# State-space layer: decay rows on 96 partitions, copied to DRAM a group at a time; the first group's TensorE order written out; a fourth state row buffer

## The chip, the cores and the metric

The kernel runs on one core of one Trainium2 chip. The metric is the device time of one execution in microseconds (us), the median over runs. Five engines work at once, each through its own instructions in order: TensorE (PE, matrix products; its weight loads are PEld), VectorE (DVE), ScalarE (ACT), GpSimd (POOL) and SyncE (SP, which issues nearly all DMAs here). An engine waits for another through semaphores.

## What is computed

The reference is a trunk of two layers, each a half-step feed-forward, a token mixer and another half-step feed-forward with normalisations. All 512 tokens have width 1024. The change lies in the mixer of the first layer, a bidirectional state-space scan over 32 heads in 4 groups of 8, in its chunked form:

```python
proj = u @ w_in
z, xbc, dt_raw = jnp.split(proj, [D_INNER, D_INNER + CONV_CH], axis=-1)
xbc = jax.nn.silu(depthwise_conv(xbc, conv_w, conv_b))
...
dt = jax.nn.softplus(dt_raw.astype(f32).reshape(b, t, 2, SSM_HEADS) + dt_bias.astype(f32))
A = -jnp.exp(a_log.astype(f32))
...
a_cs = jnp.cumsum(a, axis=-1)
L = jnp.exp(segsum(a))
CB = jnp.einsum('bclgn,bcsgn->bgcls', Cc, Bc)
y_diag = jnp.einsum('bgcls,bgjcls,bcsgjp->bclgjp', CB, L, Xc)
...
y_off = jnp.einsum('bclgn,bcgjpn,bgjcl->bclgjp', Cc, states, jnp.exp(a_cs))
```

In the kernel, a head's decay matrix L is made as exp(row + bias), where row is a cumulated decay over the tokens (one for each direction) and bias holds the same for the other token index with the log of dt. The kernel uses two chunks of 256 tokens, for both directions in one matrix E.

## The kernel before

Features lie on the 128 partitions, tokens along the free dimension. Every projection is a sum of three fp32r products (high and low parts of weights and inputs); `proj` calls `mm3`, and all their matmuls stand at L176. A projection unit of the state-space layer is 24 matmuls of 512 tokens into one PSUM bank (tile acc).

The function `ssm` has these steps, in this order.

- `dt_chain` makes the steps and cumulated decays: `pcs` (L710) is copied to `cs` (ACT, L716), `bias` (tile ssbias) is the difference (DVE, L717), four transposes (PE, L720) turn cs into rows, one for each head and direction. ACT copies 64 rows into `rows` (L722), and writes the exponentials that the state term needs into `rowe` (L724, L725). Four DMAs (L729) copy everything, for 32 heads, 16 times over into the DRAM tile `scr`.
- `prepare(g)` builds a group's shared matrices: `cb` (C times B, L796), `xt` (transposed inputs, L804 and L806), `xd` (inputs times decay, DVE, L809) and two states (PE, L813, evicted by ACT into `st`, L815).
- `ssd_head(h)` reads a head's rows back, broadcast over the partitions: `rw` (two directions, DMA at L823, two buffers) and `ch` (the state row, L825, three buffers, times C on DVE, L826). POOL masks them (L840).
- `ssd_mats(h, c)` makes E for a head and a chunk: four ACT exponentials (L848 to L851), one POOL addition (L854), one DVE multiplication by cb (L855). E has five buffers.
- `ssd_out` multiplies: three products for each of two heads into one bank (PE, tile mid, L865): two with E, one with ch and st. This is called a run below. A run appears in the trace as 12 records, since each fp32 product has two.

The loop over a group's `s` from 0 to 7 handles a pair of heads in two steps, one for each chunk: at even s it calls `ssd_head` for both heads, at each s `ssd_mats` and `ssd_out`. Between the steps it emits projection units for the next group from the list `todo` (in the first group: two convolution units for B and C, four for x, two for z), whose results ACT and DVE evict (`conv`: xc at L740, L743, L746). `last_exp` keeps an eviction xc behind the exponentials that were emitted before it.

The order on each engine is set by a scheduler that takes the emitted program, the tiles' dependences and the NOSYNC edges that the code adds. Before the change nothing ties the runs of products to a place on PE.

The text speaks of pairs 1 to 4 of the first group, each with a first run (chunk 0) and a second run (chunk 1).

Of the kernel before, what the change touches and what calls it, by code (L numbers as in the profile page):

```python
# [9 lines left out]
F32 = mybir.dt.float32  # L10
# [36 lines left out]
def hybrid_trunk(tc, xT, cb, par, cst, adaw, wgu, wdn0, wdn1, wdn2, wdt, win, wso, wqk, wv, wao, dist_in, dtp, lam_in, out):  # L47
# [114 lines left out]
    last_mm, gate = [None], [None]  # L162
# [9 lines left out]
    def mm3(o, terms, after=None, start=True):  # L172
        n, j, last = 3 * len(terms), 0, None
        for wh, wl, uh, ul in terms:
            for a, b in ((wh, uh), (wh, ul), (wl, uh)):
                last = nc.tensor.matmul(o, lhsT=a, rhs=b, start=start and j == 0, stop=j == n - 1, skip_group_check=not start)  # L176
# [473 lines left out]
    def ssm(n):  # L650
# [13 lines left out]
        scr = dp.tile([16, 32, 3, T], F32, name="scr")  # L664
# [8 lines left out]
        def dt_chain(pd):  # L673
# [41 lines left out]
            cs = tmp("cs")[:, :W]  # L715
            nc.scalar.activation(cs, pcs[:, :W], AF.Copy)  # L716
            nc.vector.tensor_tensor(out=bias.rearrange("p i h -> p (i h)"), in0=lu, in1=cs, op=ALU.subtract)  # L717
# [60 lines left out]
        def prepare(g, xs, bc):  # L778
# [19 lines left out]
            for c in range(2):  # L798
                pst = acc("ln")
                for o in range(2):  # L800
                    i = 2 * c + o
                    pp = acc("ln")
                    for k in range(4):
# [7 lines left out]
                        in1=dd[:, i, g * 8 : (g + 1) * 8].unsqueeze(2).broadcast_to([P, 8, 64]), op=ALU.mult,  # L811
# [7 lines left out]
        def ssd_head(h, Ct):  # L819

            src = scr[:, h].unsqueeze(1)
            rw = ep.tile([P, 2, T], F32, tag="rw", name="rw")
            nc.sync.dma_start(rw, src[:, :, 0:2].broadcast_to([16, 8, 2, T]))  # L823
            ch = ep.tile([P, T], F32, tag="ch", name="ch", bufs=3)
# [20 lines left out]
        def ssd_mats(h, c, rw, dx, cbs):  # L845
            E = ep.tile([P, T], F32, tag="E", name="E", bufs=NE)
            i = 2 * c
            nc.scalar.activation(E[:, :W], rw[:, 0, c * W : (c + 1) * W], AF.Exp, bias=bias[:, i, h : h + 1])  # L848
            nc.scalar.activation(E[:, W:], rw[:, 1, c * W : (c + 1) * W], AF.Exp, bias=bias[:, i + 1, 32 + h : 33 + h])
            nc.scalar.activation(dx[:, c, 0, :], dx[:, c, 0, :], AF.Exp, bias=bias[:, i, 32 + h : 33 + h])  # L850
            e = nc.scalar.activation(dx[:, c, 1, :], dx[:, c, 1, :], AF.Exp, bias=bias[:, i + 1, h : h + 1])  # L851
# [3 lines left out]
            nc.vector.tensor_tensor(out=E, in0=E, in1=cbs[c], op=ALU.mult)  # L855
            return E

        def ssd_out(pr_, c, py, mats, chs, xt, states):
            cc = slice(c * W, (c + 1) * W)
            col = [slice(pr_ * P + hh * 64, pr_ * P + (hh + 1) * 64) for hh in range(2)]  # L860
            for k in range(3):
                for hh in range(2):
                    lhs = xt[2 * c + k][:, col[hh]] if k < 2 else states[1 - c][:, col[hh]]
                    rhs = mats[hh][:, k * W : (k + 1) * W] if k < 2 else chs[hh][:, cc]
                    nc.tensor.matmul(py[hh * 64 : (hh + 1) * 64, cc], lhsT=lhs, rhs=rhs, start=k == 0, stop=k == 2)  # L865
# [59 lines left out]
        for g in range(NG):  # L925
# [263 lines left out]
def _layout(i):  # L1189
# [12 lines left out]
    def unit(w):  # L1202
# [15 lines left out]
    A["par"] = par  # L1218
    A["dtp"] = cc(np.concatenate(
        [rows(np.tile(f[k][0].reshape(-1), 4)) for k in ("ssm_dt_bias", "ssm_a_log")], axis=1  # L1220
# [26 lines left out]
    A["wdt"] = cc(w[:, 5120:].reshape(KT, P, 64).transpose(1, 0, 2).reshape(P, 512))  # L1247
# [37 lines left out]
```

## Time and profile before

| | us |
|---|---|
| median of 3 runs | 2162.59 (2161.16 to 2165.55) |
| the profiled execution, its own time | 2160.72 |
| its span | 2158.9 |
| TensorE clock granted, mean | 0.995 |

| stretch | us from the span's start |
|---|---|
| first copy of rows to DRAM issued | 416.4 |
| first masks on POOL | 436.8 |
| first exponential of a decay matrix | 444.3 |
| first run of products | 457.7 |
| first transpose for the second group | 510.3 |
| last record of the products at L865 | 750.9 |

Views of the profile give rows of this kind. A timeline row is start, length, engine, line, operation, output<-inputs, shapes, and in brackets the idle time ahead and what ended it. A chain row is start, length and work. A wait row is who waited for whom, total, times, longest. Matmuls overlap: a matmul of 512 tokens lasts 0.39 us in its row, and the next starts 0.23 us after it.

### The profile page before, as it was taken

What the parts mean: (1) busy time and instruction counts of PE and PEld (TensorE: products, weight loads), DVE (VectorE), ACT (ScalarE), POOL (GpSimd) and SP (SyncE); (2) the same over time, 40 slices, a digit from 0 to 9 for tenths busy, and PEclk for the clock granted to TensorE, in tenths of its full rate; (3) what the DMA queues carried; (4) which work ended last, traced back from release to release, by engine and by line L of the source; (5) the groups of instructions that cost most, each with busy time, mean ns of one, the idle gap of its engine ahead of it and who ended that gap; (6) DMA issues with size and microseconds to landing.
All of it is one profiled execution on the core that took longest, in us unless ns stands there. A gap on an engine that the chain in (4) does not pass through costs nothing.

```text
span 2158.9 us, 34079 instructions
## 1 busy us (share of the span) xinstructions
PE 2113.4 (98%) x13230; PEld 1854.8 (86%) x13230; DVE 1761.3 (82%) x2924; ACT 1088.2 (50%) x1824; POOL 159.5 (7%) x258
## 2 busy tenths in 40 slices
PE   7999999999999999999999999999999999999997
PEld 6889899866777698999999989899888878989897
DVE  6979998556666798989988988997777878958796
ACT  5424354757655646334456434353866647424343
POOL 0000000045333300000000000000111100000000
PEclk9999999999999999999999999999999999999999
DMA  9863635474445452636443272723322312423231
GB/s 322 307 214 113 229 120 178 102 194 139 139 135 149 119 157 79 228 124 206 152 131 118 82 260 96 258 93 112 99 69 79 89 59 69 137 78 114 73 118 40
DMA packets 90083, 301.20 MB, mean 140 GB/s; under 512 B 10048, under 2 KB 13504, under 8 KB 89920
## 3 DMA queue, kind: packets, MB, share of 16 engines
q1 hardware_dynamic: 88384, 294.81, 42.1%
q0 software_dynamic: 1536, 4.20, 0.9%
q8 instruction: 104, 1.70, 0.3%
q14 instruction: 59, 0.48, 0.1%
HBM read 289.53 MB, written 5.24 MB: 137 GB/s over the span
## 4 chain that ended last, share of the span: by engine, by line
PE 82%; DVE 7%; issue 4%; ACT 3%; DMA 2%; POOL 2%; POOLq 0%; SPq 0%; ACTq 0%; DVEq 0%
PE acc L176 66%; PE mid L176 10%; PE mid L865 2%; PE ln L176 1%; PE mid L1046 1%; DMA raw<-in_wdn 1%; DVE wl L124 1%; POOL E L854 1%; DVE raw L195 1%; DMA raw<-in_wgu 1%; ACT wh L123 1%; ACT p L1056 0%; PE ln L813 0%; PE ln L1068 0%; DVE wal L116 0%
## 5 line engine op out<-in xcount | busy, mean ns | idle before, releaser
L176 PE MATMUL acc<-hi,wh 128*128 128x256 f32 (+1 forms) x1568 | 522.5, 335 | 2.8 <-ACT hi L153 1.7
L176 PE MATMUL acc<-hi,wl 128*128 128x256 f32 (+1 forms) x1568 | 522.8, 334 | 0.0
L176 PE MATMUL acc<-lo,wh 128*128 128x256 f32 (+1 forms) x1568 | 521.8, 333 | 0.3 <-DVE lo L154 0.2
L176 PE MATMUL acc<-uh,wh 128*128 128x256 f32 (+1 forms) x1160 | 391.5, 338 | 0.0
L176 PE MATMUL acc<-ul,wh 128*128 128x256 f32 (+1 forms) x1160 | 390.4, 337 | 0.0
L176 PE MATMUL acc<-uh,wl 128*128 128x256 f32 (+1 forms) x1160 | 389.2, 336 | 0.0
L123 ACT ACTIVATE wh<-raw 128x1024 fp32r<-128x1024 f32 (+1 forms) x210 | 212.8, 1021 | 256.2 <-DMA raw<-in_wdn 100.3
L527 ACT ACTIVATE wh<-raw 128x1024 fp32r<-128x1024 f32 x198 | 209.1, 1059 | 250.6 <-PE acc L176 116.2
L176 PEld LDWEIGHTS acc<-hi,wh 128*128 128x128 f32 x1568 | 295.9, 189 | 37.5 <-ACT hi L153 4.7
L176 PEld LDWEIGHTS acc<-lo,wh 128*128 128x128 f32 x1568 | 296.1, 189 | 30.8 <-DVE lo L154 2.3
L176 PEld LDWEIGHTS acc<-hi,wl 128*128 128x128 f32 x1568 | 296.1, 189 | 29.5 <-issue 0.5
L124 DVE TENSOR_TENSOR wl<-raw,wh 128x1024 fp32r<-128x1024 f32 (+1 forms) x210 | 247.4, 1182 | 46.5 <-ACT wh L123 45.2
L528 DVE TENSOR_TENSOR wl<-raw,wh 128x1024 fp32r<-128x1024 f32 x198 | 241.0, 1219 | 22.8 <-ACT wh L527 21.9
L176 PEld LDWEIGHTS acc<-uh,wh 128*128 128x128 f32 x1160 | 219.1, 189 | 29.8 <-issue 7.4
L176 PEld LDWEIGHTS acc<-ul,wh 128*128 128x128 f32 x1160 | 219.4, 189 | 25.3 <-issue 3.9
L176 PEld LDWEIGHTS acc<-uh,wl 128*128 128x128 f32 x1160 | 219.4, 189 | 24.3 <-issue 3.0
L537 DVE TENSOR_TENSOR raw<-raw 128x512 f32<-128x512 f32 x264 | 181.3, 688 | 5.1 <-DMA raw<-in_wgu 0.4
L195 DVE SCALAR_TENSOR_TENSOR raw<-raw,cond 128x1024 f32<-128x1024 f32 x144 | 173.9, 1219 | 10.7 <-DMA raw<-in_adaw 10.6
L401 DVE SCALAR_TENSOR_TENSOR resid<-acc,gv,resid 128x512 f32<-128x512 f32 (+1 forms) x156 | 104.5, 672 | 71.2 <-PE acc L176 70.7
L341 POOL TENSOR_TENSOR rr<-vr,mhalf 128x2 f32<-128x2 f32 x12 | 9.2, 766 | 1515.5 <-DVE vr L337 1515.5
L176 PE MATMUL mid<-uh,wh 128*128 128x256 f32 (+2 forms) x332 | 99.8, 302 | 0.7 <-DVE up L569 0.7
L176 PE MATMUL mid<-uh,wl 128*128 128x256 f32 (+2 forms) x332 | 99.3, 299 | 0.0
(267 smaller groups left out, 3954.5 us busy)
## 6 DMA issues: line engine op xcount, KB each, us to landing
raw<-in_wgu SPq DMA_DIRECT2D x176, 512.0 KB, 4.1
raw<-in_adaw SPq DMA_DIRECT2D x144, 512.0 KB, 4.8
raw<-in_wdn SPq DMA_DIRECT2D x64, 448.0 KB, 4.0
raw<-in_win SPq DMA_DIRECT2D x40, 512.0 KB, 4.0
raw<-in_wdn SPq DMA_DIRECT2D x32, 512.0 KB, 4.7
rw<-scr SPq DMA_DIRECT2D x32, 512.0 KB, 5.6
ch<-scr SPq DMA_DIRECT2D x32, 256.0 KB, 3.6
raw<-in_wso SPq DMA_DIRECT2D x16, 512.0 KB, 3.7
```

What stands on the lines that cost most here:

```text
L123: nc.scalar.activation(hi[:, :n], raw, AF.Copy)
L124: nc.vector.tensor_tensor(out=lo[:, :n], in0=raw, in1=hi[:, :n].bitcast(F32), op=ALU.subtract)
L176: last = nc.tensor.matmul(o, lhsT=a, rhs=b, start=start and j == 0, stop=j == n - 1, skip_group_check=not start)
L195: nc.vector.scalar_tensor_tensor(out=raw, in0=raw, scalar=1.0, in1=cond, op0=ALU.mult, op1=ALU.mult, accum_out=mods[l][:, j : j + 1],)
L341: nc.gpsimd.tensor_tensor(out=r[:, :m], in0=vr[:, :m], in1=mhalf[:, :m], op=ALU.pow)
L401: nc.vector.scalar_tensor_tensor(out=res[d][:, a:b], in0=pd[:, a:b], scalar=gvec[n][:, d : d + 1], in1=res[d][:, a:b], op0=ALU.mult, op1=A ...
L527: nc.scalar.activation(x[0], r, AF.Copy)
L528: nc.vector.tensor_tensor(out=x[1], in0=r, in1=x[0].bitcast(F32), op=ALU.subtract)
L537: nc.vector.tensor_tensor(out=o, in0=x, in1=y, op=ALU.add)
L854: nc.gpsimd.tensor_tensor(out=dg, in0=dg, in1=dx[:, c], op=ALU.add)
L865: nc.tensor.matmul(py[hh * 64 : (hh + 1) * 64, cc], lhsT=lhs, rhs=rhs, start=k == 0, stop=k == 2)
L1046: nc.tensor.matmul(ss[m], lhsT=q[:, c], rhs=qks[h, 1][m], start=j == 0, stop=j == 1)
```

## The change

The transposes' input gets 96 columns: for each quarter of the tokens 32 columns more, a copy of the direction that the state term needs, by two DVE copies from PSUM. So one ACT exponential writes 32 rows beside the 64, all in the one tile `rows` (96 partitions), and `rowe` is gone. Heads are stored in the order that puts a group's eight on every fourth partition (`heads` in the input layout, `col(h)` in the kernel). `scr` is now four DRAM tiles, one for a group; `copy_rows(g)` issues three DMAs, for the first group in `dt_chain`, for each later one at the third pair of the group before. `ch` has four buffers.

In the first group one unit is emitted ahead of the first pair, and then two units behind every second run and none between the two runs of a pair. `hold` keeps the units behind the last product emitted; `gate` keeps the products behind the last projection emitted. In all groups, a run's first products wait until both heads' E are ready (`ready`).

```diff
-    last_mm, gate = [None], [None]
+    last_mm, gate, hold = [None], [None], [None]
...
                     tc.add_manual_dep(last.ins, after.ins.name, NOSYNC, reason="one accumulation group per bank")
+                if j == 0 and hold[0] is not None:
+                    tc.add_manual_dep(last.ins, hold[0].ins.name, NOSYNC, reason="behind the state-space products")
...
-        scr = dp.tile([16, 32, 3, T], F32, name="scr")
+        scr = [dp.tile([16, 8, 3, T], F32, name=f"scr{g}") for g in range(NG)]
+        rows = big(name="rows")
...
+            nc.vector.tensor_copy(cs[:, 0:2, 64:96], pc4[:, 0:2, 32:64])
+            nc.vector.tensor_copy(cs[:, 2:4, 64:96], pc4[:, 2:4, 0:32])
             pr = acc("ln")
             for i in range(4):
-                nc.tensor.transpose(pr[:64, i * P : (i + 1) * P], cs[:, i * 64 : (i + 1) * 64], ident)
-            rows = big(name="rows")
+                nc.tensor.transpose(pr[:96, i * P : (i + 1) * P], cs[:, i, :96], ident)
             nc.scalar.activation(rows[:64], pr[:64], AF.Copy)
-            rowe = big(name="rowe")
-            nc.scalar.activation(rowe[32:64, :W], pr[32:64, :W], AF.Exp)
-            nc.scalar.activation(rowe[0:32, W:], pr[0:32, W:], AF.Exp)
+            nc.scalar.activation(rows[64:96], pr[64:96], AF.Exp)
+            copy_rows(0)
...
-            for j, a, b, src in ((0, 0, T, rows[0:32]), (1, 0, T, rows[32:64]), (2, 0, W, rowe[32:64]), (2, W, T, rowe[0:32])):
-                nc.sync.dma_start(
-                    scr[:, :, j, a:b].rearrange("r h x -> h r x"), src[:, a:b].unsqueeze(1).broadcast_to([32, 16, b - a])
-                )
+
+        def copy_rows(g):
+            for j in range(3):
+                src = rows[j * 32 + g : j * 32 + 32 : 4].unsqueeze(1)
+                nc.sync.dma_start(scr[g][:, :, j].rearrange("r h x -> h r x"), src.broadcast_to([8, 16, T]))
+
+        def col(h):
+            return h % 8 * 4 + h // 8
...
-                        in1=dd[:, i, g * 8 : (g + 1) * 8].unsqueeze(2).broadcast_to([P, 8, 64]), op=ALU.mult,
+                        in1=dd[:, i, g : 32 : 4].unsqueeze(2).broadcast_to([P, 8, 64]), op=ALU.mult,
...
-            ch = ep.tile([P, T], F32, tag="ch", name="ch", bufs=3)
+            ch = ep.tile([P, T], F32, tag="ch", name="ch", bufs=4)
...
-            nc.vector.tensor_tensor(out=E, in0=E, in1=cbs[c], op=ALU.mult)
+            ready[c].append(nc.vector.tensor_tensor(out=E, in0=E, in1=cbs[c], op=ALU.mult))
...
+                    for x in ready[c]:
+                        if k == 0:
+                            tc.add_manual_dep(m.ins, x.ins.name, SYNC, reason="one run of products")
...
+                ready[c].clear()
+                if g == 0 and s == 0:
+                    todo[0]()
+                    done = 1
                 if c == 0:
                     heads = [ssd_head(ft * 2 + hh, Ct) for hh in range(2)]
+                    if g < NG - 1 and pr_ == 2:
+                        copy_rows(g + 1)
                     py = acc("mid")
                 mats = [ssd_mats(ft * 2 + hh, c, heads[hh][0], heads[hh][2], cbs) for hh in range(2)]
-                ssd_out(pr_, c, py, mats, [hd[1] for hd in heads], xt, states)
+                if g == 0:
+                    shut()
+                last_out = ssd_out(pr_, c, py, mats, [hd[1] for hd in heads], xt, states)
+                gate[0] = None
...
-                while done < (s + 1) * tot // 8:
+                if g == 0:
+                    hold[0] = last_out
+                while done < ((s + 1) // 2 * 2 if g == 0 else s + 1) * tot // 8 + (g == 0 and 0 < s < 7):
                     todo[done]()
                     done += 1
+                hold[0] = None
```

Three places of the order show what moves. The numbers behind the names are buffers. The first place is PE at the end of the first group's preparation; acc is a projection unit, xd times bt the last state product. Before:

```order
L176 MATMUL acc_4413<-uh_3534,wl_4410 128x512
L176 MATMUL acc_4413<-uh_3534,wh_4409 128x512
L813 MATMUL ln_4271<-xd_4289,bt_4236 128x512
L176 MATMUL acc_4413<-ul_3535,wh_4409 128x512
L176 MATMUL acc_4413<-uh_3534,wl_4410 128x512
```

Now:

```order
L176 MATMUL acc_4302<-ul_3541,wh_4298 128x512
L176 MATMUL acc_4302<-uh_3540,wl_4299 128x512
L823 MATMUL ln_4273<-xd_4291,bt_4238 128x512
L876 MATMUL mid_4367<-E_4368,xt_4256 64x256
L876 MATMUL mid_4367<-E_4375,xt_4256 64x256
L876 MATMUL mid_4367<-E_4368,xt_4266 64x256
```

Both runs of the first pair moved up to directly behind the last state product; before, 68 projection matmuls stood between.

The second place is PE at the second pair of the first group. Before, where the first run (mid_4478) begins:

```order
L176 MATMUL acc_4653<-uh_3540,wh_4649 128x512
L865 MATMUL mid_4478<-E_4479,xt_4254 64x256
L176 MATMUL acc_4653<-ul_3541,wh_4649 128x512
L176 MATMUL acc_4653<-uh_3540,wl_4650 128x512
L176 MATMUL acc_4653<-uh_3540,wh_4649 128x512
L176 MATMUL acc_4653<-ul_3541,wh_4649 128x512
L865 MATMUL mid_4478<-E_4486,xt_4254 64x256
L865 MATMUL mid_4478<-E_4479,xt_4264 64x256
```

Now, behind 48 projection matmuls in one piece:

```order
L876 MATMUL mid_4515<-E_4516,xt_4256 64x256
L876 MATMUL mid_4515<-E_4523,xt_4256 64x256
L876 MATMUL mid_4515<-E_4516,xt_4266 64x256
L876 MATMUL mid_4515<-E_4523,xt_4266 64x256
L876 MATMUL mid_4515<-ch_4481,st_4294 64x256
L876 MATMUL mid_4515<-ch_4499,st_4294 64x256
L876 MATMUL mid_4515<-E_4536,xt_4279 64x256
```

The projections that stood inside the run are gone from it, and the second run follows at once.

The third place is ACT between the first and the second pair's exponentials (E_4479 and E_4486 are the second pair's first run before, E_4516 and E_4523 after; wh is a weight's high part, xc a unit's eviction). Before:

```order
L740 ACTIVATE xc_4438<-acc_4413,pars_76 128x512
L123 ACTIVATE wh_4649<-raw_4647 128x1024
L123 ACTIVATE wh_4705<-raw_4703 128x1024
L123 ACTIVATE wh_4797<-raw_4795 128x1024
L848 ACTIVATE E_4479<-rw_4442,ssbias_3719 128x256
L849 ACTIVATE E_4479<-rw_4442,ssbias_3719 128x256
```

Now (acc_4415 and acc_4450 are the two units that stand on PE between the first and the second pair):

```order
L123 ACTIVATE wh_4594<-raw_4592 128x1024
L750 ACTIVATE xc_4440<-acc_4415,pars_76 128x512
L858 ACTIVATE E_4516<-rw_4479,ssbias_3719 128x256
L750 ACTIVATE xc_4475<-acc_4450,pars_76 128x512
L859 ACTIVATE E_4516<-rw_4479,ssbias_3719 128x256
L860 ACTIVATE dx_4484<-dx_4484,ssbias_3719 128x128
```

Both evictions of the units ahead of the second pair now stand ahead of all but one of its exponentials. In the same way the eviction of the unit emitted ahead of the first pair moved from between that pair's exponentials (before: behind the first eight) to ahead of the table load in front of them.

More of the change, by code (lines that the diff above doesn't have):

```diff
@@ L714, in dt_chain @@
                     )
-            cs = tmp("cs")[:, :W]
-            nc.scalar.activation(cs, pcs[:, :W], AF.Copy)
-            nc.vector.tensor_tensor(out=bias.rearrange("p i h -> p (i h)"), in0=lu, in1=cs, op=ALU.subtract)
+            cs = tmp("cs").rearrange("p (i q) -> p i q", i=4)
+            pc4 = pcs[:, :W].rearrange("p (i q) -> p i q", i=4)
+            nc.scalar.activation(cs[:, :, :64], pc4, AF.Copy)
+            nc.vector.tensor_tensor(
+                out=bias, in0=lu.rearrange("p (i q) -> p i q", i=4), in1=cs[:, :, :64], op=ALU.subtract
+            )
+            nc.vector.tensor_copy(cs[:, 0:2, 64:96], pc4[:, 0:2, 32:64])
+            nc.vector.tensor_copy(cs[:, 2:4, 64:96], pc4[:, 2:4, 0:32])
             pr = acc("ln")
             for i in range(4):
-                nc.tensor.transpose(pr[:64, i * P : (i + 1) * P], cs[:, i * 64 : (i + 1) * 64], ident)
-            rows = big(name="rows")
+                nc.tensor.transpose(pr[:96, i * P : (i + 1) * P], cs[:, i, :96], ident)
             nc.scalar.activation(rows[:64], pr[:64], AF.Copy)
-            rowe = big(name="rowe")
-            nc.scalar.activation(rowe[32:64, :W], pr[32:64, :W], AF.Exp)
-            nc.scalar.activation(rowe[0:32, W:], pr[0:32, W:], AF.Exp)
+            nc.scalar.activation(rows[64:96], pr[64:96], AF.Exp)
+            copy_rows(0)
             nc.scalar.activation(dd[:, 0:2, :], bias[:, 0:2, 0:32], AF.Exp)
             nc.scalar.activation(dd[:, 2:4, :], bias[:, 2:4, 32:64], AF.Exp)
-            for j, a, b, src in ((0, 0, T, rows[0:32]), (1, 0, T, rows[32:64]), (2, 0, W, rowe[32:64]), (2, W, T, rowe[0:32])):
-                nc.sync.dma_start(
-                    scr[:, :, j, a:b].rearrange("r h x -> h r x"), src[:, a:b].unsqueeze(1).broadcast_to([32, 16, b - a])
-                )
+        def copy_rows(g):
[4 more added lines that the diff above has]
+            return h % 8 * 4 + h // 8
         last_in, last_exp = [None], [None]
@@ L819, in ssd_head @@
         def ssd_head(h, Ct):
-            src = scr[:, h].unsqueeze(1)
+            src = scr[h // 8][:, h % 8].unsqueeze(1)
             rw = ep.tile([P, 2, T], F32, tag="rw", name="rw")
             nc.sync.dma_start(rw, src[:, :, 0:2].broadcast_to([16, 8, 2, T]))
-            ch = ep.tile([P, T], F32, tag="ch", name="ch", bufs=3)
+            ch = ep.tile([P, T], F32, tag="ch", name="ch", bufs=4)
             nc.sync.dma_start(ch, src[:, :, 2].broadcast_to([16, 8, T]))
@@ L847, in ssd_mats @@
             i = 2 * c
[L848 to L851, printed above, removed]
+            nc.scalar.activation(E[:, :W], rw[:, 0, c * W : (c + 1) * W], AF.Exp, bias=bias[:, i, col(h) : col(h) + 1])
+            nc.scalar.activation(E[:, W:], rw[:, 1, c * W : (c + 1) * W], AF.Exp, bias=bias[:, i + 1, 32 + col(h) : 33 + col(h)])
+            nc.scalar.activation(dx[:, c, 0, :], dx[:, c, 0, :], AF.Exp, bias=bias[:, i, 32 + col(h) : 33 + col(h)])
+            e = nc.scalar.activation(dx[:, c, 1, :], dx[:, c, 1, :], AF.Exp, bias=bias[:, i + 1, col(h) : col(h) + 1])
             last_exp[0] = e if h < 24 else None
@@ L864, in ssd_out @@
                     rhs = mats[hh][:, k * W : (k + 1) * W] if k < 2 else chs[hh][:, cc]
-                    nc.tensor.matmul(py[hh * 64 : (hh + 1) * 64, cc], lhsT=lhs, rhs=rhs, start=k == 0, stop=k == 2)
+                    m = gated(
+                        nc.tensor.matmul(py[hh * 64 : (hh + 1) * 64, cc], lhsT=lhs, rhs=rhs, start=k == 0, stop=k == 2)
+                    )
+                    for x in ready[c]:
+                        if k == 0:
+                            tc.add_manual_dep(m.ins, x.ins.name, SYNC, reason="one run of products")
+            return m
+        ready = [[], []]
         def gated_norm(g, ys, zs, fill=None):
@@ L1218, in _layout @@
     A["par"] = par
+    heads = np.arange(32).reshape(4, 8).T.reshape(-1)
+    heads = np.concatenate([heads, heads + 32])
     A["dtp"] = cc(np.concatenate(
-        [rows(np.tile(f[k][0].reshape(-1), 4)) for k in ("ssm_dt_bias", "ssm_a_log")], axis=1
+        [rows(np.tile(f[k][0].reshape(-1)[heads], 4)) for k in ("ssm_dt_bias", "ssm_a_log")], axis=1
     ))
@@ L1246, in _layout @@
     w = f["ssm_w_in"][0]
-    A["wdt"] = cc(w[:, 5120:].reshape(KT, P, 64).transpose(1, 0, 2).reshape(P, 512))
+    A["wdt"] = cc(w[:, 5120:][:, heads].reshape(KT, P, 64).transpose(1, 0, 2).reshape(P, 512))
     b = unit(w[:, :5120])
```

## The prediction

> **What bounds the kernel now.** I read the page's first part, then TensorE's waits, then the stage that the change touches in windows, and last the order of time in that stage.
>
> ```profile
> span 2158.9 us, 34079 instructions
> ```
>
> ```profile
> PE 2113.4 (98%) x13230; PEld 1854.8 (86%) x13230; DVE 1761.3 (82%) x2924; ACT 1088.2 (50%) x1824; POOL 159.5 (7%) x258
> ```
>
> TensorE (PE) is busy 98% of the span, so anything else counts only where it makes PE wait or run slowly. The waits of PE (total us, times, longest):
>
> ```profile
> PE acc L176 <- ACT wah L115: 11.3, 1, 11.3
> PE mid L865 <- DVE E L855: 5.4, 4, 4.1
> PE ln L813 <- DVE xd L809: 3.9, 5, 1.4
> ```
>
> The first is the start of the program. The second is the change's target: the products of the state-space heads (L865) wait for the decay matrices E. The first group of heads lies between its last state product (L813) and the first transpose that prepares the next group (L783). A window over all of that gives: length, then busy us of PE, PEld, DVE, ACT and POOL, the granted clock, and DMA. The groups of PE work between the two ends follow.
>
> ```profile
> 441.21:510.27 69.06, 64.34 (x288) 43.57 (x287) 40.77 (x54) 45.11 (x102) 31.93 (x55) 0.95 0.65 181
> ```
>
> ```profile
> L176 PE MATMUL acc<-ul,wh 128*128 128x512 f32 x63 | 26.0, 412 | 0.0
> ```
>
> ```profile
> L865 PE MATMUL mid<-E,xt 128*64 128x256 f32 x64 | 13.8, 426 | 4.7 <-DVE E L855 4.7
> L865 PE MATMUL mid<-ch,st 128*64 128x256 f32 x32 | 8.2, 410 | 0.0
> ```
>
> There are three projection groups of 63, so 189 matmuls (188 stand in the order behind L813), and 96 product records, which are 8 runs of 12. Prices, from the chain:
>
> ```profile
> 442.33 15.44 PE acc L176 x68
> ```
>
> ```profile
> 548.80 1.45 PE mid L865 x12
> 550.25 11.12 PE acc L176 x48
> ```
>
> 15.44/68 is 0.227 us a projection matmul, an undivided run of products is 1.45, and 48 projections with the change of kind at both ends are 11.12. The stage's own work is 188 x 0.227 + 8 x 1.45 + about 0.6 for L813 = 54.9 us. It took 69.1, so **some 14 us are lost here**. Where they go, on PE:
>
> ```profile
> 470.92 0.65 PE L865 MATMUL mid<-E,xt 128*64 128x256 f32 x2
> 471.49 0.49 PE L176 MATMUL acc<-uh,wl 128*128 128x512 f32 x1
> 471.92 0.86 PE L865 MATMUL mid<-E,xt 128*64 128x256 f32 x5
> ...
> 480.77 1.09 PE L865 MATMUL mid<-E,xt 128*64 128x256 f32 x2 [4.15 <-DVE E L855]
> ```
>
> One wait of 4.15 us; runs that begin with one head's product alone (470.92) and are broken by projections; and a slow clock behind the long wait:
>
> ```profile
> 480.60:481.60 1.00, 0.83 (x2) 0.29 (x2) 1.00 (x3) 1.00 (x5) 0.62 (x1) 0.50 0.36 127
> ...
> 485.60:486.60 1.00, 1.00 (x3) 0.82 (x3) 0.55 (x1) 0.14 (x1) 1.00 (x2) 0.50 0.63 168
> 486.60:487.60 1.00, 1.00 (x4) 0.52 (x4) 0.00 (x0) 1.00 (x4) 0.90 (x3) 0.82 0.00 0
> ```
>
> The clock is at half from 480.6 to about 487, some 6.2 us from the first matmul on, in which 3.1 us of work are lost. So 4.15 + 3.1 + small waits, and about 6 us in broken runs and changes of kind.
>
> **The change, part by part.** What it removes is the broken order: each pair's two runs are now whole, behind 48 whole projections (second place of the order). If nothing waited, nearly all 14 us would come back. What it adds decides the sign: the first two runs now stand directly behind the last state product (first place), and the 68 projections that covered their E are behind them. This is ACT, in order, for the first pair:
>
> ```profile
> 442.36 0.60 ACT L815 ACTIVATE st<-ln 128x512 f32<-128x512 f32 x1 [1.03 <-PE ln L813]
> 442.98 1.28 ACT L848 ACT_TABLE_LOAD   x1
> 444.28 0.51 ACT L848 ACTIVATE E<-rw,ssbias 128x256 f32<-128x256 f32 x1
> ...
> 445.68 0.49 ACT L848 ACTIVATE E<-rw,ssbias 128x256 f32<-128x256 f32 x1
> ...
> 447.06 0.76 ACT L740 ACTIVATE xc<-acc,pars 128x512 f32<-128x512 f32 x1
> 447.73 0.50 ACT L848 ACTIVATE E<-rw,ssbias 128x256 f32<-128x256 f32 x1
> ```
>
> ```profile
> 448.56 0.69 DVE L855 TENSOR_TENSOR E<-E,cb 128x512 f32<-128x512 f32 x1 [0.64 <-POOL E L854]
> ```
>
> ```profile
> 451.93 0.69 DVE L855 TENSOR_TENSOR E<-E,cb 128x512 f32<-128x512 f32 x1 [0.63 <-POOL E L854]
> ```
>
> ACT cannot begin the exponentials before it has evicted the last state product (st at 442.36) and loaded its table. Four instructions a head take 1.40 (444.28 to 445.68). POOL adds, DVE multiplies, and both heads' E for the first run are ready at 448.56 + 0.69 = 449.25. In the new ACT order the eviction xc of the projection unit stands ahead of the exponentials; it holds ACT 0.67 (447.06 to 447.73), so the first run begins at about **449.9** and the second run's E stays at 452.6. L813 keeps its time (441.21), since it waits for xd on DVE, which the change leaves alone:
>
> ```profile
> 441.21 1.12 PE L813 MATMUL ln<-xd,bt 128*128 128x512 f32 x2
> ```
>
> PE therefore stands from 442.3 to 449.9, **7.6 us**, and by the 4.15 us row the clock falls. At half speed the runs take 2.9 each; the second's wait vanishes in that, and both are over at 455.9. Then 48 projections: 467.0.
>
> The second pair is the third place of the order. ACT holds xc of the second of those two units in the middle of the first head's exponentials, so seven of the eight that the next run needs come only after PE has ended all 48 projections. Behind the end: 0.2 until ACT sees it (a matmul row lasts 0.39 and the next starts after 0.23), xc 0.67, the rest of a head 1.0, the other head 1.40, then POOL and DVE:
>
> ```profile
> 449.29 0.74 POOL L854 TENSOR_TENSOR E<-E,dx 128x256 f32<-128x256 f32 x1 [0.76 <-DVE E L855]
> ```
>
> 0.74 and 0.69, with about 0.25 for handovers: **4.95 us** of wait, longer than 4.15, so the clock falls again. The run starts at 471.95. The second run's E would be 2.8 later, which the slow first run (2.9) covers. Both end at 477.95; 48 projections to 489.05. For the third pair xc of the later unit stands ahead of a single small exponential: 0.2 + 0.67 + 0.4 + 0.74 + 0.69 + 0.15 = 2.85 of wait, and 0.9 before its second run; I take no fall of the clock (at most 3 us more). So 495.7, and with 48 projections 506.8. The fourth pair's exponentials do not wait behind such an eviction: two runs 2.9, then 47 projections 10.9, and the next preparation starts at 520.6 where it was 510.3. One projection matmul fewer stands ahead of it: +0.2. **Sum +10.5 us.**
>
> [...]
>
> The other edits. The two small copies into the 96 columns stand ahead of the transposes:
>
> ```profile
> 414.19 0.43 DVE L717 TENSOR_TENSOR ssbias<-E,cs 128x256 f32<-128x256 f32 x1 [3.04 <-ACT cs L716]
> ```
>
> Each is at most this long, with 64 columns rather than 256; PE has two more projections ahead of the transposes as cover (0.45), so between 0 and 0.5; I take 0.3. The copy to DRAM moves the same bytes in twelve pieces; the first group's quarter cannot be later than the whole was:
>
> ```profile
> DMA to landing us min/median/max: 13.9/14.4/14.8
> ```
>
> ```profile
> 436.81 0.78 POOL L840 TENSOR_SCALAR_AFFINE_SELECT rw<-rw 128x256 f32<-128x256 f32 x2 [57.92 <-PE ln L813]
> ```
>
> Those are the copies of rowe, issued from 417.3. Even at that pace masks begin at 436.8, ahead of the table load at 442.98: an earlier landing gains nothing, a later one has 6 us. Later quarters stand on SP ahead of the next pair's rw; rw landed within 5 us before (SP row, then POOL's):
>
> ```profile
> 448.69 1.91 SPq L823 DMA_DIRECT2D rw<-scr  x2
> ```
>
> ```profile
> 453.51 1.54 POOL L840 TENSOR_SCALAR_AFFINE_SELECT rw<-rw 128x256 f32<-128x256 f32 x2 [1.61 <-DMA rw<-scr]
> ```
>
> The second pair's exponentials now wait until 467, so 10 us hide a slower rw; I take 0, and at worst a new wait, priced below. The fourth ch buffer lets SP issue ch earlier; PE's waits, quoted above, name E and xd, not ch; 0. Strided operands (bias, dd) cost 0; if each of 16 xd products were 0.1 longer, 1.6. The other three groups keep nearly their order, and PE's waits there are the rest of the 3.9 us; 0, with 1 us either way.
>
> Total +10.8 on the profiled execution's 2160.72 us (span 2158.9 and 1.8 around it): 2171.5. The median shown, 2162.59, lies 1.9 above it, so I forecast **2173 us**.
>
> **The rivals.**
> - **Only the first wait remains.** If ACT were not held by the units' evictions, the second and third pairs would have E in time: 4.95, 2.85, 0.9 and the second fall vanish, the stage ends at about 509, and the kernel is level: 2161 to 2163. For it: masks of those pairs are done some 10 us before their exponentials start, so nothing but the place of xc holds them. Against: ACT's order has xc there, and no row shows ACT running an instruction ahead of a waiting one.
> - **The gain comes through.** If E of the first pair were ready with the state product, all waits go and 13 to 14 us are saved: 2149. Against: 442.36 to 449.25 is a chain of four engines with no slack. A partial case, the clock held, ends each of the first two pairs only 1.8 earlier, since the second runs then wait for their own E (452.6, and 2.8 behind the first); 2169 to 2170, still slower.
> - **A further wait.** If rw or a weight load of the fourth pair comes late behind the row copies on SP, one more wait like the 4.15 with its fall, 7 us: 2180. That rw is issued near 492, E is needed at 506.8, and from landing to E lie 1.54 + 1.40 + 0.74 + 0.69, so it decides once rw lands 10 us after its issue.
> - **The change does nothing**, that is, earlier rows alone matter: excluded by 436.8 against 442.98, beside the reordering.
>
> **How the numbers follow.** Forecast 0.67, with its own range 2166 to 2178 (falls that cost 0 to 3.1, copies 0 to 0.5, strides, the other groups, the third pair's clock). Level 0.14, gain 0.09, further wait 0.10. The forecast and the level case hold 0.81: range 2161 to 2178. A measurement of this kernel can tell about 0.2%, 4.3 us. Slower by more than that: 0.67 + 0.10 = 0.77; same 0.14; faster 0.09.
>
> **What would show it.** After: waits of PE products on E of about 7.6, 4.8 and 2.7 us in the first group, no broken runs there, half clock twice in it, ACT evicting xc at the end of each 48 projections, and L793 first starting near 521. The forecast is wrong if the first exponentials start before 444 or if the second pair's wait is under 2 us.

## The result and the profile after

| us | before | after |
|---|---|---|
| median of 4 runs each, same chip | 2161.88 (2159.60 to 2165.55) | 2182.51 (2179.03 to 2185.18) |
| the profiled execution, its span | 2160.72, 2158.9 | 2179.03, 2177.3 |
| first group's stage, last state product to next preparation | 69.06 | 83.59 |

The ratio is 1.0098, 95% interval 1.0086 to 1.0110: the change makes the kernel 20.6 us slower by the medians and 18.3 by the profiled executions. The prediction had +10.8, with a range that ended at 2178. One execution of c1_six_ch, a kernel further down, took 7311.81 us, and its ratio leaves it out.

First the page of the changed kernel: the span, and the engines' busy time. TensorE's busy time is 5 us lower than before while the span is 18.4 longer, so TensorE stands some 23 us more; its busy time includes the work that ran at half clock.

```profile
span 2177.3 us, 34076 instructions
...
PE 2108.3 (97%) x13230; PEld 1853.4 (85%) x13230; DVE 1766.1 (81%) x2926; ACT 1088.6 (50%) x1823; POOL 162.4 (7%) x258
```

TensorE's waits in the changed kernel: who waited for whom, total us, times, longest.

```profile
PE mid L876 <- DVE E L865: 19.6, 5, 7.6
...
PE ln L823 <- DVE xd L819: 6.3, 6, 2.6
PE ln L793 <- ACT xc L785: 5.1, 1, 5.1
```

The wait for E went from 5.4 to 19.6 (16.7 of it in this stage). The last row is new: the first transpose of the next group's preparation waits for ACT's SiLU batch. The window over the stage (length, busy us of PE, PEld, DVE, ACT, POOL, granted clock, DMA) and then, from TensorE's timeline, the places in it where it stood for 0.75 us or more, with the start of the fourth pair (507.58), where it did not:

```profile
442.86:526.45 83.59, 60.28 (x290) 43.21 (x290) 42.99 (x53) 47.12 (x106) 38.18 (x60) 0.94 0.54 157
```

```profile
451.59 1.98 PE L876 MATMUL mid<-E,xt 128*64 128x256 f32 x8 [7.61 <-DVE E L865]
...
472.56 1.98 PE L876 MATMUL mid<-E,xt 128*64 128x256 f32 x8 [5.30 <-DVE E L865]
...
490.83 1.08 PE L876 MATMUL mid<-E,xt 128*64 128x256 f32 x8 [2.78 <-DVE E L865]
...
493.37 1.08 PE L876 MATMUL mid<-E,xt 128*64 128x256 f32 x8 [1.02 <-DVE E L865]
...
496.93 0.50 PE L176 MATMUL acc<-uh,wl 128*128 128x512 f32 x1 [1.38 <-DVE wl L124]
...
507.58 1.08 PE L876 MATMUL mid<-E,xt 128*64 128x256 f32 x8
...
526.45 1.07 PE L793 MATMUL ln<-csts,xc 128*128 128x128 f32 x4 [5.14 <-ACT xc L785]
```

The runs are whole, as ordered. The first two rows' length, 1.98 where the third's is 1.08, is the half clock (0.50 granted from 451 to 454 and from 472 to 475, 1.00 from 490 to 493). Its size stands in three windows (length, PE busy, granted clock; from all engines' rows): 5 us at 0.71, 0.67 and 0.66 lose 1.5 to 1.7 us each.

```profile
452.00:457.00 5.00, 4.96 (x28) 2.59 (x25) 3.15 (x4) 0.23 (x1) 2.55 (x6) 0.71 0.76 197
472.00:477.00 5.00, 4.40 (x25) 2.15 (x26) 3.37 (x4) 1.20 (x4) 2.67 (x4) 0.67 0.76 176
...
526.00:531.00 5.00, 4.55 (x15) 3.83 (x16) 4.52 (x8) 4.98 (x9) 0.00 (x0) 0.66 0.39 150
```

Why SiLU is late stands on ACT and on SP's queue (rw loads). ACT runs in order here, and while it waits for TensorE to end a unit, exponentials behind the eviction stand still although their rows are there (the second pair's were masked by 458.92, and all but one start at 467.97 or later):

```profile
467.30 0.78 ACT L750 ACTIVATE xc<-acc,pars 128x512 f32<-128x512 f32 x1 [3.54 <-PE acc L176]
...
482.65 0.78 ACT L750 ACTIVATE xc<-acc,pars 128x512 f32<-128x512 f32 x1 [9.45 <-PE acc L176]
...
520.23 0.51 ACT L858 ACTIVATE E<-rw,ssbias 128x256 f32<-128x256 f32 x1 [3.79 <-POOL rw L850]
...
522.39 1.28 ACT L785 ACT_TABLE_LOAD   x1
```

```profile
471.30 1.90 SPq L833 DMA_DIRECT2D rw<-scr  x2
...
490.02 0.54 SPq L833 DMA_DIRECT2D rw<-scr  x1
...
503.38 1.99 SPq L833 DMA_DIRECT2D rw<-scr  x2
...
514.17 0.53 SPq L833 DMA_DIRECT2D rw<-scr  x1
```

There are two rw buffers, so a pair's rows are loaded only when the pair before it has made its exponentials. The third pair's stood behind evictions (482.65), and the last that reads its first head's rows ends at 489.96; the fourth pair's rw is issued at 490.02, the second group's first pair's at 503.38, its third head's at 514.17, 71.3 us into the stage where it was 62.9 before (504.06 less 441.21). That head's first exponential (520.23) stands on ACT ahead of the SiLU table (522.39). In the kernel before, ACT had the table first:

```profile
505.10 1.28 ACT L775 ACT_TABLE_LOAD   x1
...
516.67 0.50 ACT L848 ACTIVATE E<-rw,ssbias 128x256 f32<-128x256 f32 x1
```

So two things meet: the delay is handed from load to load to that head's rows, and its exponential now stands ahead of the SiLU batch.

### The profile page after: what moved, and what is told of

It is laid out like the page before. It is cut to its first block, busy times and chain, and to the rows that moved or that the text cites. A ratio compares the mean times of both kernels' runs of the same rounds, so it can differ in the third digit from the quotient of the medians.

```text
span 2177.3 us, 34076 instructions
## 1 busy us (share of the span) xinstructions
PE 2108.3 (97%) x13230; PEld 1853.4 (85%) x13230; DVE 1766.1 (81%) x2926; ACT 1088.6 (50%) x1823; POOL 162.4 (7%) x258
## 4 chain that ended last, share of the span: by engine, by line
PE 58%; DVE 3%; ACT 1%; issue 1%; DMA 1%; POOL 0%; POOLq 0%; ACTq 0%; SPq 0%; DVEq 0%
PE acc L176 46%; PE mid L176 8%; PE mid L1076 1%; PE ln L176 1%; PE ln L1098 0%; ACT p L1086 0%; DMA raw<-in_wgu 0%; PE ln L266 0%; PE ln L329 0%; ACT wh L123 0%; DVE p L1079 0%; DVE resid L305 0%; PE mid L325 0%; DVE raw L539 0%; POOL rr L260 0%
```

## The experiments

Theory A: all is lost by the order on TensorE and ACT, the copies and buffers cost nothing. Rival R: the row copies by group cost it. Theory B: TensorE's order alone makes every wait. An expectation below calls B the prediction's, but the prediction named ACT's order for the waits of the second and third pairs. Ratios are to the kernel before on the same chip. "Stage" is the time from the last state product to the next preparation in the profiled execution, as above; it is one execution, and the two of c1_three_rw differ by 2.5 us. The kernels c1 and c2 have some 15 projections fewer in it.

| kernel | median us | ratio, 95% | stage us |
|---|---|---|---|
| e1_rows_only | 2170.69 | 1.0048 (1.0031 to 1.0065) | 77.67 |
| e2_order_only | 2169.51 | 1.0042 (1.0026 to 1.0058) | 74.23 |
| c0_exps_first | 2162.64 | 1.0010 (1.0001 to 1.0019) | 70.16 |
| c1_cover | 2158.59 | 0.9992 (0.9983 to 1.0002) | 60.38 |
| a_silu_first | 2177.38 | 1.0078 (1.0061 to 1.0095) | 79.87 |
| c0_old_rows | 2168.62 | 1.0039 (1.0024 to 1.0054) | 74.42 |
| c0_old_rows_silu | 2160.95 | 1.0004 (0.9994 to 1.0013) | 66.05 |
| a_ch3 | 2178.67 | 1.0087 (1.0072 to 1.0102) | 80.83 |
| c1_three_rw | 2157.66 | 0.9984 (0.9975 to 0.9994) | 61.79 |
| c2_three_rw | 2166.41 | 1.0026 (1.0015 to 1.0037) | 70.17 |
| c1_six_ch | 2159.51 | 0.9994 (0.9986 to 1.0003) | 65.07 |
| c1_three_rw_again | 2156.34 | 0.9984 (0.9974 to 0.9993) | 64.24 |

### e2_order_only: the order edits without the rows

The kernel before, with `hold`, `gate`, `ready`, the unit ahead of the first pair and the new `while`:

```diff
+                if g == 0 and s == 0:
+                    todo[0]()
+                    done = 1
...
+                if g == 0:
+                    shut()
-                ssd_out(pr_, c, py, mats, [hd[1] for hd in heads], xt, states)
+                last_out = ssd_out(pr_, c, py, mats, [hd[1] for hd in heads], xt, states)
+                gate[0] = None
...
-                while done < (s + 1) * tot // 8:
+                if g == 0:
+                    hold[0] = last_out
+                while done < ((s + 1) // 2 * 2 if g == 0 else s + 1) * tot // 8 + (g == 0 and 0 < s < 7):
```

> The kernel before with the order edits alone: its rows, its one copy and three ch buffers. TensorE's order in the first group is that of the changed kernel. ScalarE's differs in one thing: the second pair's exponentials stand straight behind the first pair's, ahead of the eviction of two xc tiles and a weight split. Theory A (the loss after the first wait comes from ScalarE's order, in which exponentials stand behind work that waits for TensorE): the first pair's wait on E of 7.6 us stays, the waits of 5.3 and 2.8 us and the 5.1 us wait for the SiLU batch go, and the next preparation starts near 508.5 us; 2159 to 2164 us. Theory B (the prediction's: TensorE's order alone makes all the waits): waits as in the changed kernel, 2172 to 2183. Rival R (the copies by group cost the time): 2160 to 2170.

Measured 2169.51, between the ranges of A and B and inside R's (2160 to 2170), so the time alone decides nothing; on R, c0_exps_first decides. TensorE's timeline has two long waits in the stage, no more:

```profile
449.61 1.97 PE L868 MATMUL mid<-E,xt 128*64 128x256 f32 x8 [7.60 <-DVE E L857]
...
515.11 1.11 PE L785 MATMUL ln<-csts,xc 128*128 128x128 f32 x4 [8.11 <-ACT xc L777]
```

With TensorE's order as in the changed kernel, the waits of the second and third pairs are gone: B falls, and A's reading of them holds. But A had not seen the 8.11. ACT's timeline has its cause:

```profile
510.53 0.51 ACT L850 ACTIVATE E<-rw,ssbias 128x256 f32<-128x256 f32 x1 [5.45 <-POOL rw L842]
511.06 1.28 ACT L777 ACT_TABLE_LOAD   x1
```

The first exponential of the second group's third head waits 5.45 us for its rows ahead of the SiLU table. The load of these rows is hardly later than before (504.13, 63.3 us into the stage; 62.9 before), so here the place of that exponential alone makes the batch late.

### e1_rows_only: the rows without the order edits

The changed kernel with those order edits taken back, its rows, copies and ch buffers kept.

> Decay rows on 96 partitions, copied a group at a time, and the fourth ch buffer stay; the order of the first group is left to the scheduler again (no hold, no gate, no ready, one unit less ahead of the first pair). In the program's text the scheduler then puts three pairs of products straight one behind the other after 68 projections, where the kernel before had projections between them. Theory A (nothing is lost by the copies themselves, all by the order of TensorE and ScalarE): no delay of the group's copies, rw lands as before, and the second and third pairs wait for their E, some 4 and 13 us, so 2164 to 2172 us. Rival R (the copies by group cost the time): about 2180, with the rw loads landing later than 5 us after issue.

Measured 2170.69, in A's range. The scheduler now puts three pairs of runs in a row, and TensorE stands before the second and the third (less for the third than expected), and before the next preparation:

```profile
467.40 2.75 PE L876 MATMUL mid<-E,xt 128*64 128x256 f32 x7 [5.02 <-DVE E L865]
...
477.06 2.58 PE L876 MATMUL mid<-E,xt 128*64 128x256 f32 x7 [4.08 <-DVE E L865]
...
520.76 1.11 PE L793 MATMUL ln<-csts,xc 128*128 128x128 f32 x4 [3.60 <-ACT xc L785]
```

So this kernel doesn't isolate the rows: they move the scheduler's own order. It shows that the rows alone, with an order left free, would also have been slower.

### c0_exps_first: exponentials ahead of the evictions

All of the change stays, and TensorE's order in the stage with it. In the first group the units are called behind both chunks' `ssd_mats` of the next pair, so that `last_exp` keeps their evictions behind those exponentials:

```diff
-                if g == 0 and s == 0:
-                    todo[0]()
-                    done = 1
...
-                mats = [ssd_mats(ft * 2 + hh, c, heads[hh][0], heads[hh][2], cbs) for hh in range(2)]
+                if g > 0:
+                    mats = [ssd_mats(ft * 2 + hh, c, heads[hh][0], heads[hh][2], cbs) for hh in range(2)]
+                elif c == 0:
+                    ready[1].clear()
+                    both = [[ssd_mats(ft * 2 + hh, e, heads[hh][0], heads[hh][2], cbs) for hh in range(2)] for e in range(2)]
+                    hold[0] = last_out if s else None
+                    while done < [1, 3, 5, 7][pr_]:
+                        todo[done]()
+                        done += 1
+                    hold[0] = None
+                if g == 0:
+                    mats = both[c]
...
```

> The changed kernel with all its parts and with its TensorE order; only the place in the code where the units are called is moved, so that on ScalarE the exponentials of a pair stand ahead of the evictions of the xc tiles of the units before it. Theory A: the first wait on E stays near 6.9 us, those of 5.3, 2.8 and 1.0 us go, exponentials of the last pairs run some 15 us earlier, so the SiLU batch isn't late and the next preparation starts at 508 to 511 us; 2159 to 2165 us. Theory B (TensorE's order alone) and rival R (the copies): as the changed kernel, 2178 to 2184.

Measured 2162.64: A, and R falls, since all the copies are there. Of the stage's waits on E the first alone is left, two smaller ones for a weight split come in, and the next preparation starts without a wait, though later than the 508 to 511 expected:

```profile
451.38 1.97 PE L876 MATMUL mid<-E,xt 128*64 128x256 f32 x8 [6.93 <-DVE E L865]
...
477.64 0.50 PE L176 MATMUL acc<-uh,wh 128*128 128x512 f32 x1 [1.81 <-ACT wh L123]
...
479.41 0.79 PE L176 MATMUL acc<-uh,wl 128*128 128x512 f32 x1 [1.03 <-DVE wl L124]
...
513.48 0.66 PE L793 MATMUL ln<-csts,xc 128*128 128x128 f32 x4
```

With the same order of TensorE in the stage, ACT's order is worth some 19 us (a ratio of 1.0098 against 1.0010). Two things differ in that order: a pair's exponentials stand ahead of the evictions, and the third head's stand behind the SiLU table (509.42). The 19 us are both together, with what they move on the other engines.

### a_silu_first: the SiLU batch ahead of the second group's exponentials

One dependency for heads 8 to 11 in the changed kernel, set in the same two lines on two of a head's four exponentials:

```diff
+            if 8 <= h < 12:
+                tc.add_manual_dep(x.ins, last_silu[0].ins.name, NOSYNC, reason="SiLUs first")
```

> The changed kernel with one more dependency: the exponentials of the second group's first pair come behind the SiLU batch on ScalarE (in the changed kernel they stand ahead of it, and wait for rw loads of their own). Nothing ahead of that place is touched, so the waits on E of 7.6, 5.3, 2.8 and 1.0 us stay. Theory A (the fourth place of waiting is the SiLU batch held by those exponentials): the wait of 5.1 us at the next preparation and the fall of the clock behind it (1.7 us) go, 2173 to 2178 us. Rival (the SiLU batch is late for another reason, such as the z tiles, or the wait only moves to the second group's first products): 2179 to 2185.

Measured 2177.38, in A's range: by the ratios (1.0078 against 1.0098) some 4 us of the loss hang on these exponentials, though the intervals overlap. The first three waits on E are the same to 0.01, the fourth vanishes behind a run at half clock, and the wait for SiLU is gone:

```profile
490.68 1.97 PE L883 MATMUL mid<-E,xt 128*64 128x256 f32 x8 [2.78 <-DVE E L872]
...
521.35 0.66 PE L796 MATMUL ln<-csts,xc 128*128 128x128 f32 x4
```

The stage is only 3.7 us shorter for the 5.14, mostly because half clock cost more in this execution: 2.9 and 1.6 us behind the waits of 5.30 and 2.78, where the changed kernel lost 1.4 and nothing.

### c0_old_rows and c0_old_rows_silu: are the rows worth anything?

c0_exps_first with the rows, the copy and the three ch buffers of before; then the same with the dependency of a_silu_first.

> The kernel before with the order edits and the exponentials ahead of the evictions, so c0_exps_first with the old rows, one copy and three ch buffers. It sets the rows apart at an order that doesn't put exponentials behind evictions in either kernel. If the rows by group cost or bring nothing of their own: within 0.2% of c0_exps_first, 2158 to 2167 us, with the first wait of about 7 us in both. If the rows cost something: at least 5 us under c0_exps_first, about 2157; if they bring something: 2168 or more.

Measured 2168.62, which that expectation has under "if they bring something". The timelines of TensorE and of ACT say otherwise:

```profile
517.40 1.12 PE L785 MATMUL ln<-csts,xc 128*128 128x128 f32 x4 [9.06 <-ACT xc L777]
```

```profile
512.82 0.51 ACT L850 ACTIVATE E<-rw,ssbias 128x256 f32<-128x256 f32 x1 [6.99 <-POOL rw L842]
513.34 1.28 ACT L777 ACT_TABLE_LOAD   x1
```

As in e2_order_only, one exponential of the second group's third head, waiting 6.99 us for its rows, stands ahead of the SiLU table. In c0_exps_first the scheduler had put it behind.

> c0_old_rows (old rows, order edits, exponentials ahead of the evictions) with the dependency of a_silu_first: no exponential of the second group's second half of the first pair or later ahead of the SiLU batch. It asks why c0_old_rows was 6 us slower than c0_exps_first. Theory A (there, an exponential of the third head of the second group stands ahead of the SiLU batch and waits 7 us for its rw; the rows themselves bring nothing): the wait of 9.1 us at the next preparation goes, 2158 to 2164 us, level with c0_exps_first. Rival (rows by group are worth 6 us in themselves): stays at 2167 to 2170.

Measured 2160.95, level with c0_exps_first; the table load comes at 503.96 and the next preparation starts at 508.03 with no wait. So rows and copies neither cost nor bring anything that these runs resolve, once the order is settled (1.0004 and 1.0010, with overlapping intervals). What they did was to move the scheduler's choice of which exponential goes ahead of the SiLU batch.

### a_ch3: three ch buffers

```diff
-            ch = ep.tile([P, T], F32, tag="ch", name="ch", bufs=4)
+            ch = ep.tile([P, T], F32, tag="ch", name="ch", bufs=3)
```

> The changed kernel with three ch buffers in place of four, all else kept. TensorE's order in the first group is the same; on ScalarE a few exponentials of one pair trade places. Theory A: the fourth buffer is worth nothing here, since no product waits for ch; as the changed kernel, 2179 to 2185 us. If the fourth buffer brings or costs something: over 5 us away.

Measured 2178.67, just under A's range; its interval overlaps that of the changed kernel (1.0072 to 1.0102 and 1.0086 to 1.0110). The fourth buffer is worth nothing that these runs resolve. The comparison isn't clean: ACT's order moved too, with waits on E of 7.60, 4.50, 0.20 and 2.75 us and 2.94 for SiLU.

### c1_cover: three units ahead of the first pair

c0_exps_first with `[3, 5, 7, 8]` in place of `[1, 3, 5, 7]`.

> As c0_exps_first, but with 3, 2, 2 and 1 units of 24 projections ahead of the four pairs in place of 1, 2, 2, 2 and 1 behind the last. Theory A: the first pair is reached 10.9 us later than in c0_exps_first, so its wait of some 7 us and the fall of the clock behind it go; at most 2 to 4 us of waiting stay at the last pair; the preparation of the next group starts at 502 to 506 us, before 510.3; 2153 to 2159 us, faster than both kernels. If it is the copies that cost the time: 2165 or more.

Measured 2158.59, in A's range, but its interval holds 1. The first wait on E is gone; the next preparation starts at 503.57, with some 15 projections moved behind it (273 matmul records in the stage where c0_exps_first has 288; 3.4 us at 0.227 each). A wait for a weight split takes part of the gain:

```profile
475.51 0.80 PE L176 MATMUL acc<-uh,wh 128*128 128x512 f32 x1 [4.60 <-ACT wh L123]
```

### c1_three_rw, c1_six_ch, c2_three_rw: the wait that took its place

```diff
-            rw = ep.tile([P, 2, T], F32, tag="rw", name="rw")
+            rw = ep.tile([P, 2, T], F32, tag="rw", name="rw", bufs=3)
```

> c1_cover with a third rw buffer, so that one load of the next pair's rows doesn't wait for the exponentials of this pair. Theory A (behind the first wait, the chain exponentials, rw load, masks, exponentials holds the stage): the second and later pairs' exponentials start some 5 us earlier, the wait of 4.6 us for a weight split behind those exponentials shrinks to under 2 us; 2152 to 2158 us, faster than before. If the stage is held by the loads themselves (the DMA engines show a busy share of 0.93 to 1.04 there): as c1_cover, 2156 to 2161.

> c1_three_rw once more, in five rounds, to narrow its interval beside c1_six_ch: 2155 to 2160 us, a ratio to the kernel before of 0.997 to 1.000.

Measured 2157.66 and 2156.34, both 0.9984 with intervals that end below 1: the one version here that is faster than both kernels, by about 0.16%. The wait shrank less than expected: 3.02 for a weight's high part at 476.06, and 1.87 and 1.64 for low parts.

> c1_cover with six ch buffers in place of four, two rw buffers as before. In c1_cover and c1_three_rw the queue on SP issues no weight load between 463 and 474 us, because a ch load ahead of them waits for a buffer that the second pair's products give free; the waits of 4.6 and of 3.0 and 1.9 us for weight splits follow. Theory A' (the weight loads are held in the queue behind ch): with six buffers these waits shrink to under 2 us, the next preparation starts at 500 to 502 us, 2152 to 2156 us. Rival (the splits are late on ScalarE behind evictions and exponentials, whenever the weights land): level with c1_cover, 2157 to 2160.

Measured 2159.51: level with c1_cover, and the wait is the same 4.60. The six buffers didn't bring a weight load forward (SP's next is at 478.61, in c1_cover at 475.79), so the time alone doesn't settle it. ACT's timeline does: in c1_six_ch the split stands behind an eviction that waits for TensorE and behind a pair's exponentials that follow it, and itself starts without a wait:

```profile
471.35 0.78 ACT L750 ACTIVATE xc<-acc,pars 128x512 f32<-128x512 f32 x1 [8.87 <-PE acc L176]
...
477.55 2.00 ACT L123 ACTIVATE wh<-raw 128x1024 fp32r<-128x1024 f32 x2
```

For this split the expectation's rival holds: again ACT's order.

> c1_three_rw with 2, 2, 2 and 2 units ahead of the four pairs in place of 3, 2, 2 and 1. The first pair is reached 5.4 us earlier, so some 2 us of its wait on E come back, perhaps with a fall of the clock; in exchange ScalarE's evictions come off the second pair's path. If the waits for weight splits near 476 us hang on that order they shrink and the kernel gains 2 to 3 us (2153 to 2156); if they hang on the loads, it is level with c1_three_rw or 2 us slower (2157 to 2160).

Measured 2166.41, slower than both cases named. Two waits on E came back where one was expected, with half clock from about 451.84 to about 462.1, and the split's wait grew, all on TensorE:

```profile
451.54 1.73 PE L876 MATMUL mid<-E,xt 128*64 128x256 f32 x8 [2.01 <-DVE E L865]
...
456.67 1.97 PE L876 MATMUL mid<-E,xt 128*64 128x256 f32 x8 [2.54 <-DVE E L865]
...
480.32 0.80 PE L176 MATMUL acc<-uh,wh 128*128 128x512 f32 x1 [5.76 <-ACT wh L123]
```

## Why the prediction was wrong

Slower was right, and so was most of the mechanism; the size was short by nearly half, and the last step of the chain failed. In the profiled execution the stage began 1.65 us later than before (442.86 against 441.21). The first product of `dt_chain`, ahead of the new copies, already began 1.67 later (412.54 against 410.87), so the copies and the transposes don't make it. Over all fourteen traces the stage begins between 440.88 (e2_order_only) and 443.88 (c2_three_rw); why was not traced. Times below have 1.65 taken off.

| step, as predicted | predicted us | measured, starts less 1.65 |
|---|---|---|
| first pair's wait on E, run begins | 7.6, at 449.9 | 7.61, at 449.94 |
| second pair's wait, run begins | 4.95, at 471.95 | 5.30, at 470.91 |
| third pair's waits | 2.85 and 0.9 | 2.78 and 1.02 |
| fourth pair | none | none |
| end of the 47 projections | 520.6 | 519.66 |
| next preparation | 520.6 | 524.80 |

**What held.** The four waits for E came out within 0.4 us each, from ACT's order and the durations of the trace before. c0_exps_first shows that their cause was the one named, "ACT holds xc of the second of those two units in the middle of the first head's exponentials", for the second and third pairs, and c1_cover that the first is the lack of projections ahead of it. Copies, ch and strides at about 0 held: c0_exps_first and c0_old_rows_silu, which differ in them (and in one dependency behind the stage), have overlapping intervals.

**The step that failed** is "two runs 2.9, then 47 projections 10.9, and the next preparation starts at 520.6": it has no term for the SiLU batch. TensorE was there at 519.66, but stood 5.14 us for it. The prediction followed the delayed exponentials to the next pair's products and stopped. It did not follow them to the next rw load, which needs their buffer, and it did not ask what stands ahead of the SiLU table on ACT. It had said of rw that "10 us hide a slower rw", which was true of one pair; but each pair's delay moved the next load, and the last of these loads feeds an exponential ahead of the table. a_silu_first, with the batch put first, shows the 5.14 us gone. The place alone is enough when TensorE comes earlier: e2_order_only waits 8.11 us and c0_old_rows 9.06, with no wait on E left at the second and third pairs, and c0_old_rows_silu, with the batch first, not at all. Earlier rows with that place kept, in the changed kernel, were not tried. The rival "a further wait" had the right size of one more wait (7 us, 2180) but at another place, the fourth pair's products, and only a chance of 0.10.

**What was mis-sized.** The falls of the clock were taken at 3.1 us each, from the one row of before. They measured 1.6 and 1.4 in the stage of this execution (windows of 1 us show the half clock until 454.9 and 475.3). The prediction took the two 3 us too long in sum. (Its two pairs of slow runs are also taken at 6.0 each where 2 x 2.9 is 5.8.) But a_silu_first, behind the same wait of 5.30 us, was at half clock from the run's start at 471.00 to about 476.85 (rows of 1.98 at 471.00 and 473.86; projections 0.23 apart from 477.06) and lost 2.9, close to the prediction's 3.1. A wait of 1.38 us for a weight's low part (496.93), not foreseen, gave part of the 3 us back. So the end of the projections was right to 1 us by two errors of opposite sign, which is luck.

**What came behind the stage.** From the next preparation on, the delay grew from 16.2 to 20.2 us by the fourth group's preparation (709.26 against 689.09) and was 18.4 at the end of the span. The first 2.1 (to the last state product of the second group, 546.55 against 528.23) are about the third fall (1.7) and a longer wait for xd (0.87 against 0.28). The waits for xd in the third group's preparation are 1.5 longer (2.59 and 0.29 against 1.40). The prediction had 0 with 1 us either way. In the fourth group a wait on E of 2.87 us (763.14; 2.63 in c0_exps_first) stands where the longest was 0.72 before; `ready` makes a run wait for both heads there, but that edit wasn't tried by itself. The 1.7 us won back lie behind 1750, where the delay was still 20.1 (1770.1 against 1750.0, the same transpose): the execution before was at half clock from 1790.85 to 1794.27 with TensorE busy, a loss of 1.7, and the one after was not. That is no gain of the change.

**The rivals.** "Only the first wait remains", 2161 to 2163 if ACT is not held by the evictions, is what c0_exps_first (2162.64) did, with an edit; the changed kernel doesn't meet its condition. "The gain comes through" at 2149 was reached by no run: with all of the stage's waits on E gone, c1_cover stands for weight splits.

## What to carry to other kernels

When an instruction is delayed on an in-order engine, follow every buffer that it gives free, not only the result that it makes: here the exponentials' rw buffers carried the delay from load to load (issued at 490.02, 503.38 and 514.17). Then look at what else the delayed instruction stands ahead of on its own engine: here an exponential that waited 3.79 us for such a load stood ahead of a SiLU batch that no pair's products use. Fixing the order of one engine isn't enough where another engine's order puts waiting work (an eviction that stood 9.45 us for its unit) ahead of what the first engine needs next. Work that covers a wait has to be counted ahead of the first run as well as between the runs (a first wait of 6.93 us in c0_exps_first, none in c1_cover).

## What the runs showed of the clock

The fall of TensorE's clock doesn't go by the length of the wait alone. The third pair's wait was 2.78 us in the changed kernel and again in a_silu_first, behind the same instructions. In the first the run of eight records took 1.08 us at full clock (490.83), in the second 1.97 (490.68), and 1 us windows there show 0.50 until about 494. Even 2.01 us was followed by half clock (c2_three_rw, 451.54; 0.92 granted from 451 to 452, 0.50 in each 1 us window from 452 to 460). In c0_exps_first waits of 1.81 (477.64) and 1.03 (479.41) were too: 1.00 granted from 478 to 479, 0.60 in the next 1 us, 0.50 in the two behind it. The trace before had a fall at 480.13, in the wait of 4.15, and one at 1790.85, behind waits of 0.19 (1788.57) and 1.15 (1790.10). What sets the moment of a fall the runs don't show.

The stretches at half clock had these lengths. Before: 6.83 us from 480.13 and 3.41 from 1790.85. In the changed kernel: 6.83 from 448.03, and 3.41 from 471.92 and from 526.54. These are all in the two traces but for one in each that begins in the last 10 us of the span. In a_silu_first one lasted some 3.4, from about 490.5 (0.75 granted from 490 to 491, 0.54 from 493 to 494), and in c2_three_rw one some 10.2, from about 451.84 (projections 0.43 apart until 461.72, 0.23 from 462.12). What a fall costs is half of the part of the stretch in which there is work, by that spacing. In the changed kernel the first stretch (448.03 to 454.86) began 3.56 us ahead of the run, so only 3.3 us met work. Before, the stretch began 0.64 ahead of the run, and 6.2 us did. The changed kernel's second stretch also began 0.64 ahead, but lasted 3.41 (471.92 to 475.34); why some last 6.83 stays open.

The cost differs between executions: behind the same wait of 5.30 us the changed kernel lost 1.4 and a_silu_first 2.9. The changed kernel's four executions take longer the lower their mean clock: 2179.03 us at 0.995, 2182.23 at 0.991, 2182.79 at 0.990 and 2185.18 at 0.989. The profiled one is the first of these.
